# Preparing operands out of order, and scaling first halves on ScalarE, in a two-layer hybrid trunk

## The chip, the cores and the metric

The kernel runs on one core of one Trainium2 chip. The metric is the device time of one execution in microseconds (us). The engines are TensorE (PE, with weight loads shown as PEld), VectorE (DVE), ScalarE (ACT), GpSimd (POOL) and SyncE (SP, which here only issues transfers).

## What is computed

Two layers act on `x` of 1024 frames x 1024 channels in float32. Each layer is a mixer, a cross attention into 256 memory tokens, and a SwiGLU feed-forward block (FFN), each after an RMS norm and added to `x`:

```python
for layer in range(DEPTH):                 # 2
    h = rms_norm(x, g_mix[layer])
    x = x + (even_mixer(h, ...) if layer % 2 == 0 else odd_mixer(h, ...))
    m = rms_norm(mem, g_mem[layer])
    x = x + memory_cross_attention(rms_norm(x, g_xa[layer]), m, ...)   # 4 heads x 128
    x = x + swiglu(rms_norm(x, g_ffn[layer]), ...)                     # 1024 -> 2816 -> 1024

def swiglu(h, w_gate, w_up, w_down):
    return (jax.nn.silu(h @ w_gate) * (h @ w_up)) @ w_down
```

The even mixer joins a chunked spatial gating with a forgetting attention, the odd one a multi-scale pooling with a short gated convolution.

## The kernel before, in words

**Products.** Every float32 product is made of three PE products of a reduced type. An operand is split into a high half, cast by ACT, and a low half, the source less the high half, made by DVE in the helper `low` (L522). So each operand costs one ACT and one DVE instruction before PE can use it. The high and low halves live in `arena_r` (R), raw data in `arena_f` (F). Each arena has a region "a" and a region "b"; a string such as "ba" names the regions to try, in order.

**FFN blocks.** The FFN uses a seven-product scheme for 2 x 2 blocks. A `Unit` is one 1 MB block of weights (w_gate, w_up or w_down): one raw tile, loaded by one transfer (L225, on SP for gate and up, on POOL for down), from which seven `Part` objects are made by DVE adds (L236), ACT casts (L245) and DVE low halves (L522). Its raw tile is freed once part 6 is made. On the other side a `Pair` holds two row blocks of `x`, and its `Operand` objects are the combinations of its halves (L316 to L326, and the casts L330). They are ready only once the cross attention has added its result into `x` (L1764, a DVE addition), once `x_final` has stored the half to `xs` (L1833, on SP), squared it (L1839, L1850 or L1853 on ACT, summed by L1856 on POOL), and, for first halves, multiplied it in place by the norm's gain (L1861 on POOL, two tasks after). `collected` empties PE's banks (L1920 and L1951 on DVE, the latter in the down phase; L1922, L1928, L1930 on ACT). `gated` computes silu times the norm's scale (L1971 DVE, L1972 ACT, L1973 POOL), `upped` multiplies by the up branch (L1980 DVE), and `store` turns the result into the seven operands of the down phase (L2005 differences on POOL, L2009 casts on ACT, L522, then the transfer L2013 to the scratch tensor `pq` on SP). In the down phase those come back by L364. Gate and up run over 11 column blocks j of 256, gate then up; the last, j = 10, may only use region "b".

**What sets the order.** The program is a list of tasks. `Trunk.run` emits them one after the other and, ahead of each, prepares operands that later tasks need: in the order of their first use, as long as no more than `la` columns are ahead. The first operand that is not ready, or has no room, ends the round, whatever stands behind it. Raw tiles are fetched ahead too, while `held()`, the raw tiles whose first part is not yet made, is below `raws` (2 in gate and up, 4 and then 2 in the down phase) and `f_reserve` columns of F stay free. A scheduler then orders each engine's instructions by these priorities, so the order on an engine follows when `run` emitted them and not the time.

At the start of layer 1, `L742` (DVE) with `L741` and `L753` (ACT) and `L754` (POOL) makes the eight normed chunks of `x` that the odd mixer's projection reads, and `L640` (ACT) with `L522` prepares its weights.

In the listings below and in the diff, line numbers of the changed kernel differ: L245 is L256 there, L225 is L236, L522 is L551, L742 is L791, L1951 is L2004, L2013 is L2066, L364 is L386, L1718 and L1742 (the softmax's and the mix's casts) are L1767 and L1791, L1696 is L1745, L640 is L688, L1657 and L1661 (the queries) are L1706 and L1710.

## Time and profile before

| | |
|---|---|
| time, median of 3 | 2429.78 us (2426.87 to 2430.73) |
| profiled execution | 2428.93 us, span 2427.2 us |
| mean granted PE clock | 0.988 |
| PE busy | 2352.7 us, 97% |
| DVE busy | 1708.3 us, 70% |
| ACT busy | 1019.5 us, 42% |
| POOL busy | 752.7 us, 31% |

Times inside the profile count from the span's start. The FFN of layer 0 runs from about 650 us (its first stretch beside the end of the cross attention) to 1300, that of layer 1 from about 1720 on; the gate and up phase of layer 0 ends near 1150. PEclk is the share of the full clock that TensorE was granted in a stretch. A wait is put down to the engine and line that came last.

### The profile page before, as it was taken

The page shows a single profiled execution, that of the slowest core. Times are in us where ns is not written, and L with a number is a line of the kernel's source. Part 1 is how long each engine was busy: PE and PEld are TensorE (multiplying, and loading weights), DVE is VectorE, ACT ScalarE, POOL GpSimd, SP SyncE. Part 2 cuts the span into 40 slices and gives each one's busy share as a digit, 9 for nine tenths or more (in the row PEclk, how much of TensorE's full clock was granted, in tenths as well). Part 3 has the DMA queues.
Part 4 walks back from the last instruction along what each step waited for, and adds up shares of the span by engine and source line. Part 5 has one row for each costly group of instructions (what it writes and reads, how often), then busy time and mean ns, then how long its engine had stood idle before and what let it go on. Part 6 is the DMA issues. An engine that isn't in the chain of part 4 may idle for free.

```text
span 2427.2 us, 31163 instructions
## 1 busy us (share of the span) xinstructions
PE 2352.7 (97%) x11358; PEld 1981.8 (82%) x11358; DVE 1708.3 (70%) x2505; ACT 1019.5 (42%) x1850; POOL 752.7 (31%) x761
## 2 busy tenths in 40 slices
PE   7999999999999999998999999999989999999999
PEld 7998879888877777786888788888868777778887
DVE  5456457864888788886768653355878789878675
ACT  5345366745444344443323321145544444434221
POOL 6541233343334333432011310043433333342000
PEclk9999999999999999999999999999999999999999
DMA  7336335430224344337883121021223444347883
GB/s 231 118 131 210 97 91 136 130 123 18 100 83 148 130 156 156 130 116 248 295 271 124 53 78 52 27 68 45 105 80 137 142 145 148 122 165 257 275 286 101
DMA packets 227074, 335.57 MB, mean 138 GB/s; under 512 B 12864, under 2 KB 128664, under 8 KB 226920
## 3 DMA queue, kind: packets, MB, share of 16 engines
q1 hardware_dynamic: 214544, 289.32, 36.4%
q0 software_dynamic: 12192, 44.21, 5.2%
q8 instruction: 89, 1.46, 0.3%
q14 instruction: 65, 0.53, 0.1%
q10 hardware_dynamic: 184, 0.05, 0.0%
HBM read 226.44 MB, written 107.09 MB: 137 GB/s over the span
## 4 chain that ended last, share of the span: by engine, by line
PE 72%; DVE 12%; DMA 7%; issue 4%; POOL 2%; ACT 2%; SPq 0%; DVEq 0%; ACTq 0%; POOLq 0%
PE psum_t L510 69%; DVE arena_r L522 6%; DMA arena_f<-w_gate 2%; DMA arena_f<-w_up 2%; DMA pq<-arena_r 2%; DVE arena_f L236 1%; DVE arena_f L1920 1%; POOL arena_f L2005 1%; PE psum_t L1391 1%; DVE arena_f L1980 1%; ACT arena_r L245 1%; DMA arena_f<-e_w_in 1%; PE psum_t L1714 1%; DVE arena_f L1764 1%; DVE arena_r L742 0%
## 5 line engine op out<-in xcount | busy, mean ns | idle before, releaser
L510 PE MATMUL psum_t<-arena_r 128*128 128x512 f32 (+4 forms) x10304 | 2268.0, 379 | 57.8 <-DVE arena_r L522 25.2
L510 PEld LDWEIGHTS psum_t<-arena_r 128*128 128x128 f32 (+1 forms) x10304 | 1859.3, 190 | 413.9 <-DVE arena_r L522 41.8
L522 DVE TENSOR_TENSOR arena_r<-arena_f,arena_r 128x512 fp32r<-128x512 f32 (+4 forms) x803 | 662.8, 847 | 175.0 <-PE psum_t L510 47.2
L245 ACT CAST arena_r<-arena_f 128x512 fp32r<-128x512 f32 (+2 forms) x504 | 283.2, 583 | 422.7 <-PE psum_t L510 244.1
L1973 POOL TENSOR_TENSOR arena_f<-arena_f 128x512 f32<-128x512 f32 x88 | 164.3, 1873 | 475.2 <-ACT arena_f L1972 475.2
L236 DVE TENSOR_TENSOR arena_f<-arena_f 128x512 f32<-128x512 f32 (+2 forms) x288 | 207.7, 724 | 92.1 <-DMA arena_f<-w_down 53.2
L1920 DVE TENSOR_TENSOR arena_f<-psum_t,arena_f 128x512 f32<-128x512 f32 x208 | 141.0, 683 | 52.8 <-PE psum_t L510 33.7
L2009 ACT CAST arena_r<-arena_f 128x512 fp32r<-128x512 f32 x140 | 86.8, 621 | 161.0 <-DVE arena_f L1980 62.6
L2005 POOL TENSOR_TENSOR arena_f<-arena_f 128x512 f32<-128x512 f32 x80 | 132.2, 1672 | 46.2 <-DVE arena_f L1980 44.6
L1951 DVE TENSOR_TENSOR arena_f<-psum_t,arena_f 128x512 f32<-128x512 f32 x160 | 105.5, 683 | 41.8 <-PE psum_t L510 41.5
L640 ACT CAST arena_r<-arena_f 128x1024 fp32r<-128x1024 f32 (+1 forms) x57 | 59.0, 1043 | 111.4 <-PE psum_t L510 98.7
L522 DVE TENSOR_TENSOR arena_r<-psum_t,arena_r 128x512 fp32r<-128x512 f32 (+3 forms) x124 | 84.5, 703 | 22.1 <-ACT arena_r L1718 8.6
L754 POOL TENSOR_TENSOR arena_f<-arena_f 128x1024 f32<-128x1024 f32 x21 | 60.9, 2902 | 122.9 <-ACT arena_f L753 68.7
L1972 ACT ACTIVATE arena_f<-arena_f 128x512 f32<-128x512 f32 x88 | 55.6, 632 | 90.0 <-DVE arena_f L1971 89.8
L225 POOL DMA_DIRECT2D arena_f<-w_down x38 | 30.4, 800 | 181.3 <-DVE arena_r L522 101.8
L1381 POOL TENSOR_SCALAR arena_f<-arena_f,small 128x640 f32<-128x640 f32 (+6 forms) x64 | 48.4, 766 | 110.6 <-DVE small L1380 110.4
L1980 DVE TENSOR_TENSOR arena_f<-arena_f 128x512 f32<-128x512 f32 x88 | 72.6, 825 | 5.9 <-POOL arena_f L1973 1.8
L1971 DVE TENSOR_TENSOR arena_f<-arena_f 128x512 f32<-128x512 f32 x88 | 68.7, 781 | 4.2 <-ACT arena_f L782 4.1
L533 POOL TENSOR_TENSOR small<-small,mhalf 128x4 f32<-128x4 f32 (+1 forms) x64 | 63.5, 992 | 5.2
L1376 ACT ACTIVATE arena_f<-psum_t,small 128x640 f32<-128x640 f32 (+6 forms) x64 | 47.5, 745 | 23.7 <-DVE small L1374 20.7
L2206 POOL TENSOR_TENSOR arena_f<-arena_f 128x1024 f32<-128x1024 f32 x4 | 10.4, 2605 | 139.6 <-DVE arena_f L2158 134.8
L1930 ACT COPY arena_f<-psum_t 128x512 f32<-128x512 f32 x52 | 30.3, 584 | 55.0 <-PE psum_t L510 47.2
(192 smaller groups left out, 1549.8 us busy)
## 6 DMA issues: line engine op xcount, KB each, us to landing
pq<-arena_r SPq DMA_DIRECT2D x140, 512.0 KB
arena_r<-pq SPq DMA_DIRECT2D x280, 256.0 KB
arena_f<-w_gate SPq DMA_DIRECT2D x22, 1024.0 KB
arena_f<-w_up SPq DMA_DIRECT2D x22, 1024.0 KB
arena_r<-qk SPq DMA_DIRECT2D x48, 256.0 KB
qk<-arena_r POOLq DMA_DIRECT2D x16, 512.0 KB, 4.2
arena_f<-xa_wkv SPq DMA_DIRECT2D x16, 512.0 KB
arena_f<-xs SPq DMA_DIRECT2D x16, 512.0 KB
```

The costliest lines, as they stand in the source:

```text
L236: getattr(T.nc, self.adds).tensor_tensor(out=out, in0=a, in1=b, op=what)
L245: T.nc.scalar.copy(out=hv, in_=src)
L510: self.nc.tensor.matmul(out=out, lhsT=lhsT, rhs=rhs, start=start, stop=stop, skip_group_check=again)
L522: getattr(self.nc, eng).tensor_tensor(out=out, in0=src, in1=high, op=ALU.subtract)
L533: self.nc.gpsimd.tensor_tensor(out=out, in0=in_, in1=self.mhalf[:, 0:in_.shape[-1]], op=ALU.pow)
L1920: nc.vector.tensor_tensor(out=o, in0=bank[q].ap, in1=o if other is None else other, op=ALU.add)
L1951: nc.vector.tensor_tensor(out=o, in0=bank[q].ap, in1=o, op=ALU.add)
L1971: nc.vector.tensor_tensor(out=q, in0=q, in1=r, op=ALU.mult)
L1973: nc.gpsimd.tensor_tensor(out=q, in0=q, in1=r, op=ALU.mult)
L1980: nc.vector.tensor_tensor(out=c[j].ap[:, o], in0=c[j].ap[:, o], in1=s.ap[:, o], op=ALU.mult)
L2005: nc.gpsimd.tensor_tensor(out=out, in0=a, in1=b, op=ALU.subtract)
L2009: nc.scalar.copy(out=t.ap[:, 0:512], in_=src)
```

## The change

`run` no longer prepares strictly in order. `choose` takes the operand that is due, or else the first of the next 64 that is ready; an operand that is not ready is passed over. Columns of parts made ahead are limited to `parts_max`, 4608. An age test (`self.age`) is there too; every assignment in the program sets it to 0. Raw tiles are counted in `live` from their load until they are freed, and `raws` is 3 (in the down phase 4, then 3). After the cross attention's last use of the normed input, `parts_early` widens `la` to 9216 and sets `f_reserve` to 3072. The first gate and up blocks (j = 0) may put their parts in region "a" first. The scaling of first halves is an ACT activation with a scale (line 1914) in place of POOL's L1861.

```diff
@@ Part (other operand classes: aged = 0, loaded returns i)
+    aged = 1
+
+    def loaded(self, i):
+        at = self.unit.parts[0].fetched
+        return i if at is None else at
...
@@ Unit.make
         if i == 6:
             self.raw.free()
             self.tmp.free()
+            T.live -= 1
@@ Trunk
+        self.age = self.live = self.parts = 0
+        self.parts_max = 4608
@@ Trunk.run
-        def held():
-            return sum(w.heavy for w in order[npre:nd])
+        def fetch_ahead(i):
+
+            for w in pending[:160]:
+                if w.fetched is not None:
+                    continue
+                if w.heavy and self.live >= self.raws:
+                    break
+                if w.fetch(self, False):
+                    w.fetched = i
+                    self.live += w.heavy
+                elif w.ready():
+                    break
+
+        def choose(i):
+            if pending and pending[0].first <= i:
+                return pending[0], True
+            for w in pending[:64]:
+                if w.ready() and i - w.loaded(i) >= self.age * w.aged and self.parts + w.cols * w.aged <= self.parts_max:
+                    return (w, False) if ahead + w.cols <= self.la else (None, False)
+            return None, False
+
         for i, t in enumerate(self.tasks):
             self.settle()
             while True:
-                need = npre < len(order) and order[npre].first <= i
-                if not need and not (npre < len(order) and ahead + order[npre].cols <= self.la):
+                w, need = choose(i)
+                if w is None:
                     break
-                w = order[npre]
-                if not w.ready():
-                    assert not need, ("not ready", i)
-                    break
...
@@ cross attention
+        def parts_early():
+            self.la, self.f_reserve, self.age = 9216, 3072, 0
+
...
                     self.add(free_all)
+                    self.add(parts_early)
@@ x_final
         def scale():
-            nc.gpsimd.tensor_scalar(out=x, in0=x, scalar1=pr.g[e], scalar2=1.0, op0=ALU.mult, op1=ALU.mult)
+            nc.scalar.activation(out=x, in_=x, func=AF.Copy, scale=pr.g[e])
             pr.lo[e] = True
         self.defer(scale, 2)
@@ ffn
-            self.reserve, self.raws = 0, 2
+            self.reserve, self.raws = 0, 3
             self.f_reserve = 4096
...
-            g = Unit(wg, [(0, 4)], 4, j * 256, "b" if j == 10 else "ba")
-            u = Unit(wu, [(0, 4)], 4, j * 256, "b" if j == 10 else "ba")
+            g = Unit(wg, [(0, 4)], 4, j * 256, "b" if j == 10 else "ba", "ba" if j else "ab")
+            u = Unit(wu, [(0, 4)], 4, j * 256, "b" if j == 10 else "ba", "ba" if j else "ab")
...
             if n == 1:
-                self.add(lambda: setattr(self, "raws", 2))
+                self.add(lambda: setattr(self, "raws", 3))
```

The instructions of both programs are the same in number and kind, but for the sixteen scalings; what changes is where they stand. Three places follow.

First, ACT at the end of layer 0's cross attention, where the first weight parts of the FFN are cast. Before, the first of these casts (L245) stand behind the last softmax rows (L1696):

```order
L1718 CAST arena_r<-psum_t 128x1024
L1696 ACTIVATE arena_f,small<-psum_t,small 128x256 x4
L1742 CAST arena_r<-psum_t 128x512
L1718 CAST arena_r<-psum_t 128x1024
L245 CAST arena_r<-arena_f 128x512 x3
L1742 CAST arena_r<-psum_t 128x512
L1718 CAST arena_r<-psum_t 128x1024
L245 CAST arena_r<-arena_f 128x512
L1850 ACTIVATE arena_f<-arena_f 128x512
L245 CAST arena_r<-arena_f 128x512
L1853 ACTIVATE arena_f<-arena_f 128x512
```

Now nine of them (L256) stand ahead of the last softmax rows (L1745):

```order
L256 CAST arena_r<-arena_f 128x512 x5
L1706 ACTIVATE arena_r<-psum_t,gc 128x512
L688 CAST arena_r<-arena_f 128x1024
L256 CAST arena_r<-arena_f 128x512
L1791 CAST arena_r<-psum_t 128x512
L1710 ACTIVATE arena_f<-psum_t 128x512
L1767 CAST arena_r<-psum_t 128x1024
L256 CAST arena_r<-arena_f 128x512
L1745 ACTIVATE arena_f,small<-psum_t,small 128x256 x4
L256 CAST arena_r<-arena_f 128x512 x2
L1791 CAST arena_r<-psum_t 128x512
L1745 ACTIVATE arena_f,small<-psum_t,small 128x256 x4
```

The nine parts have moved ahead by about two of the softmax's row blocks; their low halves on DVE moved with them.

Second, SP at the end of gate and up in layer 0, where the last w_gate and w_up blocks are loaded among the stores to `pq`. Before:

```order
L2013 DMA pq<-arena_r 128x2x512 x11
L225 DMA arena_f<-w_gate 128x8x256
L2013 DMA pq<-arena_r 128x2x512 x7
L225 DMA arena_f<-w_up 128x8x256
L364 DMA arena_r<-pq 128x512 x110
```

Now:

```order
L2066 DMA pq<-arena_r 128x2x512 x12
L236 DMA arena_f<-w_gate 128x8x256
L2066 DMA pq<-arena_r 128x2x512 x3
L236 DMA arena_f<-w_up 128x8x256
L2066 DMA pq<-arena_r 128x2x512 x3
L386 DMA arena_r<-pq 128x512
```

Between the last two weight loads three stores are left of seven.

Third, DVE at the start of layer 1, where the sixth, seventh and eighth chunks of the normed input (L742, now L791) stand among the last evacuations of the down phase (L1951, now L2004) and the low halves of the odd mixer's weights (128x1024). Before:

```order
L522 TENSOR_TENSOR arena_r<-arena_f,arena_r 128x1024 x2
L1951 TENSOR_TENSOR arena_f<-psum_t,arena_f 128x512 x2
L522 TENSOR_TENSOR arena_r<-arena_f,arena_r 128x1024
L742 SCALAR_TENSOR_TENSOR arena_r<-arena_f,gc,arena_r 128x8x128
L1951 TENSOR_TENSOR arena_f<-psum_t,arena_f 128x512
L742 SCALAR_TENSOR_TENSOR arena_r<-arena_f,gc,arena_r 128x8x128
L522 TENSOR_TENSOR arena_r<-arena_f,arena_r 128x1024
L742 SCALAR_TENSOR_TENSOR arena_r<-arena_f,gc,arena_r 128x8x128
```

Now, from the fifth chunk on:

```order
L551 TENSOR_TENSOR arena_r<-arena_f,arena_r 128x1024 x2
L2004 TENSOR_TENSOR arena_f<-psum_t,arena_f 128x512
L551 TENSOR_TENSOR arena_r<-arena_f,arena_r 128x1024
L2004 TENSOR_TENSOR arena_f<-psum_t,arena_f 128x512
L791 SCALAR_TENSOR_TENSOR arena_r<-arena_f,gc,arena_r 128x8x128
L2004 TENSOR_TENSOR arena_f<-psum_t,arena_f 128x512 x2
L791 SCALAR_TENSOR_TENSOR arena_r<-arena_f,gc,arena_r 128x8x128
L551 TENSOR_TENSOR arena_r<-arena_f,arena_r 128x1024
L2004 TENSOR_TENSOR arena_f<-psum_t,arena_f 128x512
L791 SCALAR_TENSOR_TENSOR arena_r<-arena_f,gc,arena_r 128x8x128 x2
```

One low half of 1024 columns has moved to a place ahead of the seventh chunk here, and one more further up; the eighth chunk now follows the seventh directly.

More of the change, by code (lines that the diff above doesn't have):

```diff
@@ L546, in run @@
                     order.append(w)
-        nd = npre = 0
+        pending = order
+        for w in order:
+            w.fetched = None
         ahead = 0
-        def held():
-            return sum(w.heavy for w in order[npre:nd])
+        def fetch_ahead(i):
[16 more added lines that the diff above has]
+            return None, False
         for i, t in enumerate(self.tasks):
@@ L570, in run @@
                     break
-                npre += 1
+                pending.remove(w)
                 ahead += w.cols
-                while nd < len(order) and held() < self.raws and order[nd].fetch(self, False):
-                    nd += 1
-            while nd < len(order) and held() < self.raws and order[nd].fetch(self, False):
-                nd += 1
+                self.parts += w.cols * w.aged
+                fetch_ahead(i)
+            fetch_ahead(i)
             self.urgent(t.fn, t.boost)
@@ L580, in run @@
                     ahead -= w.cols
+                    self.parts -= w.cols * w.aged
                     w.first = -1
@@ L2070, in down_start @@
             self.x = [None] * KD
-            self.reserve, self.la, self.f_reserve, self.raws = 0, 4096, 2048, 4
+            self.reserve, self.la, self.f_reserve, self.raws, self.age = 0, 4096, 2048, 4, 0
         self.add(down_start)
@@ L2119, in down_end @@
         def down_end():
-            self.la, self.reserve = 3072, 0
+            self.la, self.reserve, self.age = 3072, 0, 0
         for n, (mp, lo, hi) in enumerate(VISITS):
@@ L2131, in ffn @@
             if n == 1:
-                self.add(lambda: setattr(self, "raws", 2))
+                self.add(lambda: setattr(self, "raws", 3))
+            if n == 3:
+                self.add(lambda: setattr(self, "age", 0))
             if 5 <= n < 9:
```

19 lines of the change are left out of this document (17 added, 2 removed).

## The prediction

> **What bounds the kernel now.** I read the page first: what share of the span TensorE (PE) is busy, and the chain that ended last.
>
> ```profile
> span 2427.2 us, 31163 instructions
> PE 2352.7 (97%) x11358; PEld 1981.8 (82%) x11358; DVE 1708.3 (70%) x2505; ACT 1019.5 (42%) x1850; POOL 752.7 (31%) x761
> PE psum_t L510 69%; DVE arena_r L522 6%; DMA arena_f<-w_gate 2%; DMA arena_f<-w_up 2%; DMA pq<-arena_r 2%; DVE arena_f L236 1%; DVE arena_f L1920 1%; POOL arena_f L2005 1%; PE psum_t L1391 1%; DVE arena_f L1980 1%; ACT arena_r L245 1%; DMA arena_f<-e_w_in 1%; PE psum_t L1714 1%; DVE arena_f L1764 1%; DVE arena_r L742 0%
> ```
>
> PE is the bound, and the change takes no matmul away, so only time that PE loses can be won. The second view, busy time by stretches of 50 us, says where it loses any.
>
> ```profile
> core 0: us, PE busy (x) PEld busy (x) DVE busy (x) ACT busy (x) POOL busy (x), PEclk, DMA share, GB/s
> 550.00:600.00 50.00, 50.00 (x290) 43.80 (x289) 21.88 (x35) 27.53 (x68) 16.25 (x35) 1.00 0.07 22
> 600.00:650.00 50.00, 50.00 (x253) 42.43 (x253) 39.75 (x61) 23.26 (x47) 15.37 (x24) 1.00 0.23 79
> 650.00:700.00 50.00, 46.86 (x218) 39.03 (x218) 45.15 (x56) 24.13 (x43) 26.75 (x19) 0.90 0.26 90
> 700.00:750.00 50.00, 47.35 (x197) 37.58 (x196) 43.00 (x58) 25.23 (x43) 19.68 (x11) 0.97 0.40 137
> 750.00:800.00 50.00, 50.00 (x222) 41.41 (x221) 41.37 (x58) 21.37 (x38) 16.75 (x9) 1.00 0.36 127
> 1050.00:1100.00 50.00, 44.42 (x190) 36.05 (x189) 39.02 (x52) 20.56 (x37) 18.90 (x13) 0.96 0.46 163
> 1100.00:1150.00 50.00, 46.69 (x197) 36.89 (x197) 34.86 (x61) 21.94 (x45) 12.83 (x12) 0.97 0.69 239
> 1300.00:1350.00 50.00, 47.71 (x208) 38.51 (x206) 46.34 (x62) 28.21 (x39) 17.64 (x7) 1.00 0.22 64
> 1350.00:1400.00 50.00, 48.22 (x208) 38.98 (x209) 28.67 (x22) 9.72 (x16) 13.36 (x16) 0.97 0.15 47
> 1700.00:1750.00 50.00, 48.52 (x234) 40.36 (x233) 42.76 (x58) 23.91 (x44) 23.29 (x20) 0.98 0.20 74
> 1750.00:1800.00 50.00, 45.92 (x193) 35.79 (x192) 38.87 (x53) 23.54 (x39) 15.54 (x11) 0.88 0.24 75
> 2150.00:2200.00 50.00, 43.64 (x178) 34.36 (x178) 37.96 (x60) 21.14 (x41) 18.10 (x13) 0.93 0.65 224
> ```
>
> An undisturbed stretch (750 to 800) holds 222 matmuls, 0.225 us each. What a stretch loses I count as its idle PE time plus (1 - PEclk) x 50 us. In 2150 to 2200 that is 6.36 + 3.5 = 9.9 us, and the 44 missing matmuls give 44 x 0.225 = 9.9 too. So: FFN opening of layer 0 (650 to 750) 3.14 + 5.0 + 2.65 + 1.5 = 12.3 us; its end (1050 to 1150) 5.58 + 2.0 + 3.31 + 1.5 = 12.4; opening of layer 1 (1700 to 1800) 1.48 + 1.0 + 4.08 + 6.0 = 12.6; its end 9.9. The start of layer 1 (1300 to 1400) loses 2.29 + 1.78 + 1.5 = 5.6. The change touches all five; the first four, 47.2 us, are the most it can win. Who is waited for, over the whole span, then in 650 to 750 and in 1700 to 1800:
>
> ```profile
> PE psum_t L510 <- DVE arena_r L522: 25.2, 27, 2.1
> PE psum_t L510 <- DVE arena_f L1920: 8.7, 2, 4.4
> ...
> PE psum_t L510 <- DVE arena_r L522: 3.4, 2, 2.1
> ...
> PE psum_t L510 <- DVE arena_r L522: 3.5, 3, 1.4
> ```
>
> In the openings it is mostly the low halves (L522) on a VectorE (DVE) that is busy 45.15 and 43.00 of 50 us, and had 28.1 idle us in 550 to 600 and 10.3 in 600 to 650. That is work made too late, not too much work.
>
> **Openings.** By the listing of the order, nine weight parts of the FFN are cast among the cross attention's softmax, where three were by the same row, so six move out of the crowded stretch; the cap of 4608 columns is nine parts of 512. Eight scalings per layer go from GpSimd (POOL) to ScalarE (ACT).
>
> ```profile
> L522 DVE TENSOR_TENSOR arena_r<-arena_f,arena_r 128x512 fp32r<-128x512 f32 x65 | 55.3, 873 | 5.6 <-ACT arena_r L2009 2.6 <-ACT arena_r L245 1.0 <-PE psum_t L510 0.8
> ...
> L236 DVE TENSOR_TENSOR arena_f<-arena_f 128x512 f32<-128x512 f32 x24 | 18.0, 758 | 5.8 <-DMA arena_f<-w_gate 5.7
> ...
> L1853 ACT ACTIVATE arena_f<-arena_f x14: 624/630/633, 638.0 to 1738.8; 128x512 f32<-128x512 f32 x14
> ...
> L1861 POOL TENSOR_SCALAR arena_f<-arena_f,gc x16: 691/1136/1662, 638.8 to 1741.4; 128x512 f32<-128x512 f32 x16
> ...
>   DMA xs<-arena_f: 0.5, 1
> ...
>   ACT arena_r L330: 8.3, 9
> ```
>
> Six parts are six low halves of 0.87 us and, with four adds to seven parts, 3.4 adds of 0.76: 7.8 us of DVE time moved ahead, into 38 us of idle time. That is more than the 3.4 us for which PE waits on L522 there (and 3.5 in layer 1), so I take those waits as gone. Half of the lost clock I give to them, since the slow steps follow clusters in which waits on ACT stand too: 3.4 + 6.5/2 = 6.6 us, and 3.5 + 7.0/2 = 7.0 us in layer 1. Bounds: nothing, if DVE stays as slow as its 0.87 us mean here, and 12.3 and 12.6. The scalings cost ACT 8 x 0.63 (an ACT instruction of this size, L1853) = 5.0 us a layer, while six casts leave; ACT idles 25 of 50 us there, and on POOL they took 1.1 us with casts (L330) behind them waiting 8.3 us in all. I cost them at nothing. Without that cover they would cost up to 5.0 us a layer.
>
> The clock needs a second look, by 10-us stretches:
>
> ```profile
> 680.00:690.00 10.00, 8.66 (x34) 7.44 (x35) 9.32 (x13) 4.75 (x9) 4.22 (x3) 0.66 0.01 2
> ...
> 1090.00:1100.00 10.00, 5.63 (x20) 4.28 (x19) 5.01 (x9) 1.58 (x3) 2.55 (x3) 0.81 0.99 337
> ...
> 1770.00:1780.00 10.00, 6.06 (x17) 3.74 (x16) 9.14 (x14) 3.38 (x6) 5.17 (x3) 0.77 0.00 0
> ```
>
> In 680 to 690 only 1.34 us are idle and yet the granted clock is 0.66; in 1090 to 1100, 4.37 idle us leave 0.81. The Trainium skill, "TensorE: Matmul & The Clock Gate", section "HAM oscillation — how this bites in real kernels", asks only that no gap exceeds some 3.4 us. By that, the short waits of the openings would cost no clock, and mending them would give none back: 6.9 us there in place of 13.6. The row of 680 to 690 speaks against it, the one of 1090 to 1100 agrees.
>
> **End of the gate and up phase.** The last w_up shares its raw tile with the last w_gate, before and after.
>
> ```profile
> 1066.62 0.37 SPq L225 DMA_DIRECT2D arena_f<-w_gate  x1
> ...
> 1092.60 1.98 SPq L225 DMA_DIRECT2D arena_f<-w_up  x1
> ...
> 1080.05 7.05 POOL L2005 TENSOR_TENSOR arena_f<-arena_f 128x512 f32<-128x512 f32 x4 [10.37 <-DVE arena_f L1980]
> ...
> 1087.13 1.14 ACT L2009 CAST arena_r<-arena_f 128x512 fp32r<-128x512 f32 x2 [0.51 <-POOL arena_f L2005]
> ...
> 1103.37 2.18 ACT L245 CAST arena_r<-arena_f 128x512 fp32r<-128x512 f32 x4 [3.10 <-DMA arena_f<-w_up]
> ...
> 1096.31 0.43 DVE L236 TENSOR_TENSOR arena_f<-arena_f 128x256 f32<-128x256 f32 x1 [4.56 <-DMA arena_f<-w_down]
> ...
> 1097.39 5.49 PE L510 MATMUL psum_t<-arena_r 128*128 128x512 f32 x12 [4.37 <-DVE arena_f L1920]
> 1104.04 3.22 PE L510 MATMUL psum_t<-arena_r 128*128 128x512 f32 x12 [1.16 <-ACT arena_r L245]
> ```
>
> DVE stands 4.56 us before an add that waits for w_down; L1920, which empties PE's bank, is queued behind it, and PE loses 4.37 us. w_up is issued at 1092.60 and used 10.8 us later. The gate's last cast stands behind ACT's L2009, which waits for POOL's four L2005 (7.05 us). In the new order that cast is not behind them, and three pq stores instead of seven stand ahead of w_up on SP. So w_up is issued up to 7.05 us earlier; it needs 4.37 + 1.16 = 5.5 us for its wait to stay hidden once the other is gone. Counted in the order of both programs, 80 matmuls (18 us) lie between what releases the first w_down loads and their use, instead of 47 (10.6 us). I take the long wait and its clock as gone, and 1.5 us (about the 1.16 us row) as what stays: 4.37 + 2.0 - 1.5 = 4.9 us; layer 1, with the same wait: 4.3 + 3.5 - 1.5 = 6.3. Together 11.2, bounds 2 (w_up comes hardly earlier) and 22.3 (all of both ends). The new order also puts POOL's L1973 ahead of those L2005; the pq stores behind those end later, and are read only in the down phase.
>
> **What is late next.** At the start of layer 1, two more low halves of 1024 columns stand on DVE ahead of the seventh L742, for which PE waits already:
>
> ```profile
> 1350.89 3.40 DVE L522 TENSOR_TENSOR arena_r<-arena_f,arena_r 128x1024 fp32r<-128x1024 f32 x1
> ...
> 1351.02 4.53 PE L510 MATMUL psum_t<-arena_r 128*128 128x512 f32 x12 [3.17 <-DVE arena_r L742]
> ```
>
> Such a low half takes up to 3.40 us beside a POOL instruction, and DVE has 3.7 idle us in 1300 to 1350 to take some of it: 0 to 6.8, and I take 3.5 us, one of them. In the tails of both cross attentions the parts made early now stand ahead of what PE's small pieces need (15 to 19 matmuls, 4 us, of lead). I charge 1.5 us each, between one and two waits of 25.2/27 = 0.93 us; bounds 0 and 5 for both. The steady middle I leave at nothing: the order keeps 49 to 65 matmuls (11 us or more) between what releases a w_up load and its use, against the 10.8 us of the slowest load.
>
> **Sum.** Against the profiled run of 2428.93 us: -6.6 - 7.0 - 11.2 + 3.5 + 3.0 = -18.3, so 2410.6. The median shown is 0.85 higher, and I say 2411. All bounds together give 2382 and 2439.
>
> **Rivals.**
> - *The clock does not come back.* The slow steps of the openings belong to something other than those waits. Then 6.75 of the 13.6 us stay: 2417. For it: 0.66 with 1.34 idle us; against it: no stretch without idle time is under 1.00. The rule of the Trainium skill named above comes out here. Chance 0.10.
> - *DVE stays the bound of the openings.* 88 of 100 us are busy; less 7.8 still 80, next to POOL, and the waits on L522 only change places: ends 11.2, losses 6.5, 2424. For it: PE's waits on L522 are spread over the whole span (27 of them), where none of this work stands. Chance 0.20.
> - *The change does less than it says.* The two last loads still share a tile, the new age test is never above zero, and the count of raw tiles is capped by space too: ends give 2, not 11.2: 2420. Chance 0.12.
> - *Slower.* SP now issues a third 1 MB load ahead of the sixteen stores to xs. Each scaling overwrites what a store reads, and sits on ACT ahead of L330's casts and the last mix's cast; POOL once waited 0.5 us for this and delayed nobody on ACT. If the stores wait for half of a 10.8 us load in each layer, the openings' 13.6 are lost and 2 x 5.4 come on top: 2435. It decides from some 3 us of delay. Against it: DMA is 0.23 busy there. Chance 0.09.
> - *All four places are mended*, 47.2 less 6.5: 2388. Chance 0.09.
>
> **How the numbers follow.** The forecast has 0.40, with 2403 to 2418 as its own range. From 2395 (most of the last case is outside) to 2429 (the slower case is outside) holds about 0.8. A measurement tells 0.2%, 4.9 us, from no change, so faster means under 2424.9. That holds for nearly all of the forecast, the clock rival and the full mending (0.57), half of the DVE rival and most of the lesser change: 0.78. Same 0.14, slower 0.08.
>
> **What would show it.** Right: in the stretches that hold the openings DVE's busy time falls by some 8 us, in the softmax stretch it rises, PEclk there is 0.95 or more; no wait on L1920 over 2 us; w_up issued 5 us or more sooner after the last w_gate than 26 us. Right for the loss: the wait on L742 is over 5 us. The forecast is wrong if PE waits on ACT's casts in the openings, if the scalings on ACT (line 1914 of the changed kernel) begin after a wait on xs, or if the down phase waits on w_down again.

## The result, and the profile after

The changed kernel takes 2389.92 us (median of 5, 2385.24 to 2391.95), the kernel before, on the same chips, 2426.87 (2424.17 to 2430.73): a ratio of 0.9846, 95% interval 0.9836 to 0.9857, some 37 us less. The prediction was 2411 us, with 2395 to 2429 as its range: the right direction, about half of the size, and the time lies 5 us under the range.

The page of the profile after, its span and busy times:

```profile
span 2388.1 us, 31149 instructions
PE 2337.4 (98%) x11358; PEld 1976.5 (83%) x11358; DVE 1705.6 (71%) x2505; ACT 1024.2 (43%) x1866; POOL 743.0 (31%) x745
```

The same 11358 matmuls stand in a span that is 39 us shorter. TensorE's (PE's) waits over the whole span, in the changed kernel (L551 is the low half, L1973 the emptying of a bank in gate and up, L791 the chunks of the odd mixer's input, L256 the cast of weight parts):

```profile
PE psum_t L539 <- DVE arena_r L551: 10.7, 15, 2.7
...
PE psum_t L539 <- DVE arena_r L791: 6.2, 2, 5.3
PE psum_t L539 <- ACT arena_r L256: 3.6, 3, 1.7
...
PE psum_t L539 <- DVE arena_f L1973: 1.5, 1, 1.5
```

The waits for low halves fell from 25.2 us to 10.7, those for the emptying of banks from 8.7 to 1.5, and the ones for the chunks rose from 3.2 to 6.2. Busy times by stretches, of the changed kernel:

```profile
550.00:600.00 50.00, 50.00 (x291) 43.80 (x289) 25.28 (x40) 27.57 (x65) 17.03 (x37) 1.00 0.13 43
...
650.00:700.00 50.00, 50.00 (x240) 41.64 (x239) 45.06 (x61) 30.45 (x52) 19.68 (x13) 0.93 0.22 78
700.00:750.00 50.00, 48.92 (x216) 40.19 (x215) 46.26 (x58) 22.35 (x40) 17.78 (x11) 1.00 0.41 144
...
1050.00:1100.00 50.00, 48.00 (x203) 38.73 (x202) 41.59 (x69) 23.64 (x47) 18.59 (x16) 0.97 0.73 255
1100.00:1150.00 50.00, 50.00 (x222) 41.40 (x222) 39.67 (x65) 21.33 (x40) 11.04 (x11) 1.00 0.80 269
...
1300.00:1350.00 50.00, 43.43 (x186) 34.54 (x185) 34.94 (x35) 14.80 (x16) 16.19 (x6) 0.93 0.25 74
```

VectorE's (DVE's) columns are the third pair. In 550 to 600 it does 3.4 us more than before. In 650 to 750 it is as busy as before (91.3 of 100 us, against 88.2): the stretch did not empty, it came to hold work that belonged later.

Both programs have the same number of PE instructions, and almost the same order, so the time between the same two of them can be compared. The table gives, for each part of the program, the profiled time less that of the kernel before (us; negative is a gain). "Start" is the part ahead of the first cross attention's tail, where all the programs are the same: its -0.3 to -5.3 is what two profiles of the same code differ by, most of it in waits for the first loads. The other parts should be read to about 1 or 2 us. The tail of layer 1 (predicted +1.5) and the last down phase have no column; they moved by nothing and by +1.2 us in the changed kernel.

| kernel | median | start | tail, layer 0 | opening 0 | steady 0 | end 0 | start of layer 1 | opening 1 | steady 1 | end 1 |
|---|---|---|---|---|---|---|---|---|---|---|
| predicted | 2411 | 0 | +1.5 | -6.6 | 0 | -4.9 | +3.5 | -7.0 | 0 | -6.3 |
| changed | 2389.92 | -2.3 | +2.5 | -10.4 | -6.6 | -8.8 | +4.1 | -10.6 | -6.6 | -1.4 |
| a_strict | 2427.08 | -0.3 | +0.1 | -0.3 | +0.3 | -2.4 | +3.2 | -6.3 | +5.9 | -2.0 |
| a_only | 2403.68 | -0.6 | +1.9 | -4.5 | -9.0 | -0.7 | -0.3 | -4.2 | -5.9 | +0.3 |
| b_scale | 2417.35 | -1.5 | 0.0 | -5.9 | -1.6 | +0.1 | -1.7 | -4.0 | +0.7 | +1.1 |
| a_noscale | 2391.54 | -5.3 | +1.1 | -5.7 | -8.2 | -9.3 | +4.9 | -8.6 | -6.4 | -2.2 |
| b_raws3 | 2429.89 | -0.6 | 0.0 | +2.1 | -4.3 | +5.2 | -0.1 | -0.9 | -10.4 | +7.8 |
| a_raws2 | 2402.23 | -2.4 | +0.8 | -8.1 | -7.9 | -1.6 | +3.9 | -8.6 | -2.2 | -0.4 |
| a_raws4f | 2388.90 | -3.2 | +0.4 | -9.4 | -4.4 | -5.0 | +3.4 | -11.9 | -9.0 | -3.0 |
| a_noearly | 2395.56 | -2.0 | +0.4 | -8.1 | -8.2 | -1.1 | +3.1 | -10.7 | -7.0 | -4.8 |
| a_early3 | 2464.57 | -1.0 | +1.5 | -6.5 | +18.2 | +3.2 | +4.7 | -2.5 | +9.3 | +6.5 |
| a_twice | 2431.51 | -1.4 | +1.1 | -9.2 | +9.6 | -5.6 | +4.0 | -9.5 | +14.4 | -3.2 |
| a_down | 2388.91 | -1.3 | +2.4 | -10.6 | -7.9 | -6.2 | +3.8 | -7.4 | -7.0 | -3.4 |
| a_spread1 | 2405.39 | -3.7 | +1.9 | -3.2 | -5.8 | -4.8 | +3.5 | -7.5 | -2.4 | -3.3 |
| a_sqv | 2376.79 | -0.5 | +2.3 | -10.6 | -7.8 | -9.0 | -2.7 | -13.4 | -6.7 | -3.5 |
| b_sqv | 2426.48 | -5.3 | 0.0 | -0.1 | -1.5 | -0.1 | -2.0 | -0.6 | +1.7 | -0.3 |

Names with a_ are the changed kernel with one thing altered, names with b_ the kernel before. The first row of results says where the prediction missed: the two openings gave 21.0 us where 13.6 were forecast, the two steady stretches 13.2 where nothing was, and the end of layer 1 gave 1.4 where 6.3 was.

### The profile page after: what moved, and what is told of

Same layout as the page of the kernel before. It is cut to its first block, busy times and chain, and to the rows that moved or that the text cites. A ratio compares the mean times of both kernels' runs of the same rounds, so it can differ in the third digit from the quotient of the medians.

```text
span 2388.1 us, 31149 instructions
## 1 busy us (share of the span) xinstructions
PE 2337.4 (98%) x11358; PEld 1976.5 (83%) x11358; DVE 1705.6 (71%) x2505; ACT 1024.2 (43%) x1866; POOL 743.0 (31%) x745
## 3 DMA queue, kind: packets, MB, share of 16 engines
q8 instruction: 89, 1.46, 0.3%
## 5 line engine op out<-in xcount | busy, mean ns | idle before, releaser
L539 PE MATMUL psum_t<-arena_r 128*128 128x512 f32 (+4 forms) x10304 | 2255.4, 378 | 34.2 <-DVE arena_r L551 10.7
L551 DVE TENSOR_TENSOR arena_r<-arena_f,arena_r 128x512 fp32r<-128x512 f32 (+4 forms) x803 | 672.1, 857 | 167.5 <-PE psum_t L539 53.2
L256 ACT CAST arena_r<-arena_f 128x512 fp32r<-128x512 f32 (+2 forms) x504 | 282.4, 584 | 429.4 <-PE psum_t L539 252.6
L1973 DVE TENSOR_TENSOR arena_f<-psum_t,arena_f 128x512 f32<-128x512 f32 x208 | 141.7, 685 | 51.6 <-PE psum_t L539 36.0
L2004 DVE TENSOR_TENSOR arena_f<-psum_t,arena_f 128x512 f32<-128x512 f32 x160 | 106.4, 686 | 36.0 <-PE psum_t L539 35.7
L803 POOL TENSOR_TENSOR arena_f<-arena_f 128x1024 f32<-128x1024 f32 x21 | 60.6, 2884 | 127.8 <-ACT arena_f L802 61.9
L551 DVE TENSOR_TENSOR arena_r<-psum_t,arena_r 128x512 fp32r<-128x512 f32 (+3 forms) x124 | 84.6, 703 | 18.7 <-ACT arena_r L1443 6.8
L2261 POOL TENSOR_TENSOR arena_f<-arena_f 128x1024 f32<-128x1024 f32 x4 | 10.4, 2598 | 139.5 <-DVE arena_f L2213 139.5
L1753 POOL TENSOR_SCALAR arena_f<-arena_f,small 128x256 f32<-128x256 f32 x64 | 33.3, 538 | 65.2 <-DVE small L1750 50.8
```

The costliest lines, as they stand in the source:

```text
L256: T.nc.scalar.copy(out=hv, in_=src)
L539: self.nc.tensor.matmul(out=out, lhsT=lhsT, rhs=rhs, start=start, stop=stop, skip_group_check=again)
L551: getattr(self.nc, eng).tensor_tensor(out=out, in0=src, in1=high, op=ALU.subtract)
L1973: nc.vector.tensor_tensor(out=o, in0=bank[q].ap, in1=o if other is None else other, op=ALU.add)
L2004: nc.vector.tensor_tensor(out=o, in0=bank[q].ap, in1=o, op=ALU.add)
```

## The experiments

### Passing over: a_strict and a_only

In a_strict operands are prepared strictly in order again, and everything else of the change stays.

```diff
-            for w in pending[:64]:
+            for w in pending[:1]:
```

> The changed kernel, but operands are prepared strictly in the order of their first use again: one that is not ready blocks all behind it. Theory A and the prediction's reading of the openings: the six parts go back into the crowded stretch, the openings lose 13 to 22 us, the steady stretches keep their gain by the third raw tile: 2403 to 2412. Theory B: the openings lose as much and the steady stretches lose 10 to 13 us with them: 2415 to 2425. A third reading (widening the columns that are prepared ahead, and the third raw tile, did it all, and passing over does nothing): 2388 to 2393.

It took 2427.08 us, 1.0001 of the kernel before (0.9991 to 1.0012): without passing over, nothing is left of the change in all. The opening of layer 0 has its loss back, and the steady stretches lose their gain with three raw tiles in place; the opening of layer 1 keeps 6.3 of its 10.6 us. None of the three readings had the sum, and the one of Theory B (below) came nearest.

The opposite test is a_only: passing over with the other edits undone. The bookkeeping that came with it (raw tiles counted until they are freed, the cap of 4608 columns) stays in both tests and has none of its own.

```diff
-            nc.scalar.activation(out=x, in_=x, func=AF.Copy, scale=pr.g[e])
+            nc.gpsimd.tensor_scalar(out=x, in0=x, scalar1=pr.g[e], scalar2=1.0, op0=ALU.mult, op1=ALU.mult)
...
-                    self.add(parts_early)
...
-            self.reserve, self.raws = 0, 3
+            self.reserve, self.raws = 0, 2
...
-            g = Unit(wg, [(0, 4)], 4, j * 256, "b" if j == 10 else "ba", "ba" if j else "ab")
+            g = Unit(wg, [(0, 4)], 4, j * 256, "b" if j == 10 else "ba")
...
-                self.add(lambda: setattr(self, "raws", 3))
+                self.add(lambda: setattr(self, "raws", 2))
```

> Passing over alone: the changed kernel with the scalings on GpSimd, two raw tiles in gate and up and after the first visit of the down phase, no widening of the columns ahead before the tail, and the first blocks' parts placed as before. If passing over carries the change (strict order gave 2427), it keeps the openings' gain in good part: 2400 to 2410. If it needs the other edits as they need it (each alone was worth 0 to 9.7 us), it stays near the kernel before: 2418 to 2428.

2403.68 us, ratio 0.9911 (0.9891 to 0.9932): more than half of the gain, from 4 us in each opening and all of the steady stretches. So passing over carries more than half of the change; a_strict has all the rest of it and gains nothing.

### The scaling: b_scale and a_noscale

```diff
-            nc.gpsimd.tensor_scalar(out=x, in0=x, scalar1=pr.g[e], scalar2=1.0, op0=ALU.mult, op1=ALU.mult)
+            nc.scalar.activation(out=x, in_=x, func=AF.Copy, scale=pr.g[e])
```

b_scale does this alone to the kernel before.

> The kernel before with only the sixteen scalings of first halves moved from GpSimd to ScalarE. The prediction's reading (they cost nothing and win nothing by themselves): 2425 to 2429. Rival (part of the openings' gain of 21.6 us came from GpSimd and from casts that no longer wait 8.3 us for it): each opening gains 3 to 5 us, 2417 to 2421.

2417.35 us, ratio 0.9960 (0.9944 to 0.9976): the sixteen scalings, which the prediction had cost at nothing, win 9.3 us by the medians, and by the table 5.9 and 4.0 us in the openings. a_noscale puts the scalings of the changed kernel back on GpSimd (POOL).

> The changed kernel with the sixteen scalings put back on GpSimd. If the scaling's 9.7 us in the kernel before (2417 against 2427) are a gain of its own that adds to the rest, both openings lose 4 to 6 us: 2398 to 2401. If passing over reaches the same by another way (parts made early leave room for whatever waits on GpSimd), little is lost: 2389 to 2394. The prediction's reading, that the scaling wins nothing, says the same as the latter.

2391.54 us (2389.66 to 2394.8), 0.9863 (0.9848 to 0.9878): only 1.6 us more than the changed kernel, or some 4 by the ratios to the kernel before, which the intervals do not tell apart. By the table the openings do lose 4.7 and 2.0 us; 1.6 us come back in the steady stretch of layer 0, and this profile's start is 3 us shorter, which is no part of the edit. The two gains do not add.

### How early the parts are made: a_noearly and a_early3

a_noearly leaves out the task that widens the columns prepared ahead (the line `self.add(parts_early)`).

> The changed kernel without the step that widens the columns prepared ahead to 9216 after the last use of the normed input; the width stays at 3072 until the tail of the cross attention. The prediction's reading of the openings (gain from work moved into the idle time of the softmax) needs this step: most of what passing over wins there goes, 5 to 6 us a layer, and the tail of layer 0 gets its 2.5 us back: 2397 to 2400. Rival: passing over alone is enough: 2388 to 2392.

2395.56 us, 0.9876 (0.9862 to 0.9891). The sum is near what the prediction's reading gave, the place is not: the openings kept 8.1 and 10.7 us, and what went is the end of layer 0 (-1.1 in place of -8.8). So that step is not what mends the openings. It does not decide whether parts are made early either: in its trace five and nine weight parts are cast ahead of the last softmax row in layers 0 and 1 (none and one before, nine and seven in the changed kernel). The profile, 2.6 us slower than the median, also has 7.7 us of loss in the last down phase, where the changed kernel has 1.2.

a_early3 allows three parts ahead (1536 columns), as many as stood there before, until the steady stretches begin.

```diff
-        self.parts_max = 4608
+        self.parts_max = 1536
...
         def steady():
-            self.reserve, self.la = 3072, 2048
+            self.reserve, self.la, self.parts_max = 3072, 2048, 4608
...
             if left == 1:
                 self.add(down_end)
+                self.add(lambda: setattr(self, "parts_max", 1536))
```

> The changed kernel with at most 1536 columns (three parts, as many as the kernel before has at that row) prepared ahead until the steady stretches of gate and up begin, and 4608 from there on. The prediction's reading (the openings gain because six parts move into the idle time of the softmax): the openings lose 10 to 14 us of their 21: 2400 to 2406. Rival (what counts is that an operand that is not ready no longer blocks those behind it, and how early the parts are made counts little): 2389 to 2394.

Both sides missed the time: 2464.57 us, 1.0165 (1.0148 to 1.0181), slower than before. The openings gained 6.5 and 2.5 us, 12.0 less than in the changed kernel, which is what the prediction's reading expected there, so fewer parts ahead do cost; but the large loss, 18.2 and 9.3 us, is in the steady stretches, where the cap is lifted. VectorE waited 28.9 and 15.6 us there for weights to land. The order in which blocks are fetched at the start of the steady stretch stays with it for most of its length: here, on SyncE, a w_up load, one store, a w_gate load and then six stores stood in this order, again and again, where the changed kernel mostly has two to five stores behind each load.

### The steady stretches: a_raws2, b_raws3, a_raws4f, a_twice

After the result I had two theories. Theory A: blocks land earlier, since three raw tiles are held, and VectorE's adds wait less. Theory B: the steady stalls before were the aftermath of a late opening. What VectorE waited for in the steady stretch of layer 0, before:

```profile
DVE arena_f L236 <- DMA arena_f<-w_gate: 10.9, 4, 4.9
...
DVE arena_f L236 <- DMA arena_f<-w_up: 3.3, 2, 2.8
```

and in the changed kernel (no such wait for w_up):

```profile
DVE arena_f L247 <- DMA arena_f<-w_gate: 7.5, 3, 3.5
```

How such a wait reaches PE is seen at the longest stall of that stretch, in the kernel before, on VectorE, then PE:

```profile
838.94 1.42 DVE L236 TENSOR_TENSOR arena_f<-arena_f 128x512 f32<-128x512 f32 x2 [4.90 <-DMA arena_f<-w_gate]
840.28 0.68 DVE L522 TENSOR_TENSOR arena_r<-arena_f,arena_r 128x512 fp32r<-128x512 f32 x1
...
841.01 13.89 PE L510 MATMUL psum_t<-arena_r 128*128 128x512 f32 x60 [1.91 <-DVE arena_r L522]
```

The low half that PE waits for stands on VectorE behind an add that waited 4.90 us for its block.

a_raws2 is the changed kernel with two raw tiles, b_raws3 the kernel before with three.

```diff
-            self.reserve, self.raws = 0, 3
+            self.reserve, self.raws = 0, 2
```

> The changed kernel with two raw weight tiles at a time in gate and up instead of three; they are still counted until they are freed. Theory A (the steady stretches of gate and up gained 6.6 us in layer 0 and 6.0 us in layer 1 because the weights of the next block land earlier): both stretches fall back, so 2390 + 10 to 14, about 2402, and VectorE waits again for w_gate in its adds by 10 us or more per layer. Theory B (the steady stalls before were the aftermath of late openings): the steady stretches keep their gain, and the time stays within 2388 to 2393. In both the openings keep their gain, since nine parts need two raw tiles only.

> The kernel before with three raw tiles instead of two in gate and up, nothing else changed. Theory A: the steady stretches gain 10 to 13 us in all, 2427 - 12 = about 2415. Theory B: the openings are as late as before, so nothing follows: 2424 to 2430.

a_raws2 took 2402.23 us, 0.9892 (0.9877 to 0.9907), which is the number of Theory A, by another way: the steady stretch of layer 0 kept its gain (VectorE waited 2.5 us for weights), that of layer 1 lost most of it (11.8 us), and the end of layer 0 lost 7.2. b_raws3 took 2429.89 us, 1.0011 (1.0000 to 1.0023), which is the number of Theory B, again by another way: the steady stretches gained 4.3 and 10.4 us, with waits of 4.5 and 1.5, and the ends lost 5.2 and 7.8. A median alone would have misled twice; the parts of the table say that the third tile matters for the landing in layer 1, and that theory B is wrong: in b_raws3 the openings are as late as before, and the steady stretches gain all the same.

a_raws4f holds four tiles and keeps less space free.

```diff
-            self.reserve, self.raws = 0, 3
-            self.f_reserve = 4096
+            self.reserve, self.raws = 0, 4
+            self.f_reserve = 2048
```

> The changed kernel with four raw weight tiles in gate and up and only 2048 columns of space kept free. If the steady stretches are set by VectorE adds that wait for weights (in the six kernels so far each us less of these waits went with some 0.8 us less time in the same stretch), the waits fall from 7.5 and 5.1 us to under 3 in each layer and the steady stretches gain 2 to 6 us more. The last w_gate and w_up again have seven stores between them in layer 0, so its end loses 4 to 7 us: 2388 to 2394 in all, with the gain in the steady stretches and the loss at the ends. Rival (the steady gain has nothing to do with the weights' landing): the steady stretches stay as they are or lose, 2394 to 2400.

2388.90 us, 0.9854 (0.9837 to 0.9870), the same as the changed kernel. The end of layer 0 lost 3.8 us, near the 4 to 7 expected, and layer 1's steady stretch won 2.4; but in layer 0 VectorE waited 17.7 us for weights, not under 3, and the stretch still was 4.4 us better than before. So the waits are not the whole of it, and in that one case they hardly show.

a_twice therefore delays the landing: from the second block on, the last left out, each load is issued twice.

```diff
-            getattr(T.nc, self.queue).dma_start(
+            for _ in range(2 if self.queue == "sync" and 256 <= self.c0 < 2560 else 1):
+                getattr(T.nc, self.queue).dma_start(
```

> The changed kernel, but each weight block of gate and up from the second on, the last left out, is loaded twice into its raw tile, the second load over the first. If the steady stretches gained because VectorE's adds wait less for weights to land, later landing brings the waits back (from 7.5 and 5.1 us to 12 us and more) and with them 4 to 12 us in each steady stretch: 2398 to 2412. If the steady gain has another cause (the openings, or the order alone), the stretches stay within 3 us: 2387 to 2394.

2431.51 us, 1.0030 (1.0016 to 1.0043). The steady stretches lost 16.2 and 21.0 us against the changed kernel, more than expected, and the rest of the table stayed within 4. VectorE's waits in that stretch of layer 0:

```profile
DVE arena_f L248 <- DMA arena_f<-w_gate: 29.0, 6, 7.3
...
DVE arena_f L248 <- DMA arena_f<-w_up: 1.3, 2, 0.7
```

Over the two steady stretches of all sixteen kept traces, 32 in number, each us of VectorE's waits for weights goes with 0.8 us of time (correlation 0.91). So the landing time is the best account of these stretches: an add waits for a block, and the low halves and the emptying of banks behind it are what PE is seen to wait for. It is not isolated, though. In a_twice VectorE's order changed too (at 174 of the 318 places of layer 0's stretch it runs another kind of instruction than the changed kernel), stores to pq stand between the doubled loads, and a_raws4f's layer 0 lies some 7 us under the line.

### The start of layer 1: a_down, a_sqv, b_sqv

a_down goes back to two raw tiles after the down phase's first visit, which puts VectorE's order there back to what it was before.

```diff
             if n == 1:
-                self.add(lambda: setattr(self, "raws", 3))
+                self.add(lambda: setattr(self, "raws", 2))
```

> The changed kernel with two raw tiles instead of three in the down phase after its first visit, as before. In the order of VectorE four low halves of 1024 columns stand ahead of the seventh chunk of the odd mixer's input, as before, instead of six. The prediction's reading of the loss there: the wait goes from 5.3 us back to 3.2 and the second half-clock step goes: 2390 - 4 = 2385 to 2387. Rival: the third raw tile also fed the down phase, which loses as much: 2389 to 2393.

2388.91 us, 0.9856 (0.9839 to 0.9872): no difference. The wait on the seventh chunk fell from 5.3 to 3.6 us, but other waits came, both half-clock steps stayed, and the part lost 3.8 us as the changed kernel does (this profile is 7 us slower than the median of its runs). So the two low halves made that wait longer, and do not by themselves make the part slow. The changed kernel there, on VectorE, then GpSimd and PE:

```profile
1308.40 1.22 DVE L551 TENSOR_TENSOR arena_r<-arena_f,arena_r 128x1024 fp32r<-128x1024 f32 x1
...
1322.32 3.40 DVE L551 TENSOR_TENSOR arena_r<-arena_f,arena_r 128x1024 fp32r<-128x1024 f32 x1
...
1326.24 6.07 DVE L791 SCALAR_TENSOR_TENSOR arena_r<-arena_f,gc,arena_r 128x1024 fp32r<-128x1024 f32 x2
...
1321.30 9.93 POOL L803 TENSOR_TENSOR arena_f<-arena_f 128x1024 f32<-128x1024 f32 x3 [4.17 <-ACT arena_f L802]
...
1329.07 3.35 PE L539 MATMUL psum_t<-arena_r 128*128 128x512 f32 x7 [5.29 <-DVE arena_r L791]
```

The same low half takes 1.22 us alone and 3.40 beside GpSimd's additions (L803, 9.93 us for three). Those add up the squares for the norm, which is not needed yet. a_sqv moves these seven additions to VectorE.

```diff
-    def chunk_sq(self, k):
+    def chunk_sq(self, k, eng="gpsimd"):
...
-            nc.gpsimd.tensor_tensor(out=self.ssq.ap, in0=self.ssq.ap, in1=sq.ap, op=ALU.add)
+            getattr(nc, eng).tensor_tensor(out=self.ssq.ap, in0=self.ssq.ap, in1=sq.ap, op=ALU.add)
...
-                        self.chunk_sq(k)
+                        self.chunk_sq(k, "vector")
```

> The changed kernel with the seven additions of squares (1024 columns, 3.3 us each on GpSimd) of the odd mixer's norm moved to VectorE (1.2 us each by its other instructions of that size). In the profile of the changed kernel a VectorE instruction of 1024 columns takes 1.2 us alone and 2.8 to 3.4 beside one of those additions. If the wait of 5.3 + 0.9 us at the start of layer 1 comes from that overlap, it falls below 3 us, one half-clock step goes with it: 2390 - 5 = 2383 to 2387. If it comes from the two more low halves on VectorE, as the prediction had it, seven more instructions there make it longer: 2392 to 2397.

2376.79 us (2375.06 to 2378.3), 0.9797 (0.9780 to 0.9815): faster than both kernels. The two waits on L791 are 1.55 and 0.43 us, and no half-clock step is left there. VectorE in its profile:

```profile
1317.90 1.21 DVE L803 TENSOR_TENSOR arena_f<-arena_f 128x1024 f32<-128x1024 f32 x1
1319.04 2.47 DVE L791 SCALAR_TENSOR_TENSOR arena_r<-arena_f,gc,arena_r 128x1024 fp32r<-128x1024 f32 x2
1321.43 1.21 DVE L551 TENSOR_TENSOR arena_r<-arena_f,arena_r 128x1024 fp32r<-128x1024 f32 x1
```

Two chunks take 2.47 us where they took 6.07. The part itself won 6.8 us; of the rest, 4.9 us are in the opening and end of layer 1, where VectorE's order changed too. Each of the two has one half-clock step less there (those from 1722 and 2156 us in the changed kernel), 3.4 us in all; why was not tested. b_sqv does the same to the kernel before.

> The kernel before, with only the seven additions of squares at the start of layer 1 moved from GpSimd to VectorE. If their overlap with VectorE's 1024-column instructions is a cause by itself, the kernel before loses its wait of 3.2 us on the seventh chunk and its half-clock step there too: 4 to 7 us less, 2417 to 2420. If it needs the two more low halves of the changed kernel to show, the kernel before stays at 2422 to 2427.

2426.48 us, 1.0003 (0.9992 to 1.0015): no difference, though its profile shows that part 2.0 us shorter (it was 3.2 us of wait, and one of 0.8 stayed). The overlap costs at most 2.0 us in the kernel before and 6.8 us in the changed one; what differs between them there is the order, so it seems to take both: the additions on GpSimd, and the low halves that the new order puts beside them.

### The clock of the openings: a_spread1

The changed kernel, by 10-us stretches:

```profile
660.00:670.00 10.00, 10.00 (x47) 8.42 (x48) 9.96 (x12) 4.41 (x9) 4.73 (x4) 0.83 0.14 53
...
680.00:690.00 10.00, 10.00 (x41) 8.19 (x41) 8.92 (x15) 4.26 (x8) 5.38 (x3) 0.83 0.01 2
```

PE is busy in all of both, and yet the granted clock is 0.83. Just ahead of each stands a lot of one-column matmuls, which sum squares:

```profile
658.38 2.82 PE L539 MATMUL psum_t<-ones,arena_f 128*128 128x1 f32 x24
...
677.96 2.73 PE L539 MATMUL psum_t<-ones,arena_f 128*128 128x1 f32 x24
```

a_spread1 defers these matmuls one by one, which puts them into lots of other sizes.

```diff
-            self.defer(sums)
+            for b in range(4):
+                self.defer(lambda b=b: sums(b), 1 + b)
```

> The changed kernel with the four one-column matmuls of each channel block's sum of squares deferred one by one; in TensorE's order they then stand in lots of 5, 4, 4 and 23 in layer 0, instead of 12, 4, 8 and 12. If the half-clock steps of the opening come from waits, as the prediction had it, the opening of layer 0 keeps its two steps or fewer (6.8 us at half clock). If they come from lots of one-column matmuls, in which TensorE counts as busy and hardly works, the lot of 23 (some 5 us) brings two steps or more right behind it and with no wait ahead of them, and the lots of 4 and 5 bring none.

One execution: 2405.39 us, 15 us slower than the changed kernel, which the table puts mostly into the openings, the end of layer 0 and the steady stretch of layer 1. The lot of 23 (46 entries in the trace, two for each matmul):

```profile
675.12 8.66 PE L539 MATMUL psum_t<-ones,arena_f 128*128 128x1 f32 x46
```

and the stretches around it:

```profile
660.00:670.00 10.00, 10.00 (x49) 8.36 (x49) 8.65 (x12) 4.73 (x8) 2.73 (x2) 1.00 0.07 27
670.00:680.00 10.00, 8.21 (x42) 6.69 (x41) 8.89 (x10) 5.21 (x9) 4.84 (x4) 0.84 0.32 105
680.00:690.00 10.00, 10.00 (x39) 8.78 (x40) 9.71 (x15) 4.08 (x8) 5.48 (x4) 0.65 0.01 2
```

The clock is halved from 677 to 687 us, three steps in a row, and the lot of 4 at 667.58 brought none. In layer 1 the lot of 23 (from 1746.20 us) brought three steps too. Waits of 1.46 and 1.14 us stand just ahead of these two, so they are not free of waits; but the two lots of the changed kernel above are.

Yet not every such lot halves the clock. a_twice has the same two lots, and keeps the full clock in all of its opening of layer 0:

```profile
659.50 2.73 PE L540 MATMUL psum_t<-ones,arena_f 128*128 128x1 f32 x24
...
660.00:670.00 10.00, 10.00 (x59) 8.71 (x60) 9.96 (x15) 7.01 (x13) 3.39 (x3) 1.00 0.19 72
...
676.60 2.73 PE L540 MATMUL psum_t<-ones,arena_f 128*128 128x1 f32 x24
...
680.00:690.00 10.00, 7.41 (x30) 5.18 (x29) 8.10 (x13) 3.56 (x7) 5.53 (x4) 1.00 0.10 32
```

The clock records of the sixteen kept traces show the difference. In each trace all half-clock steps begin a whole number of 3.41 us apart, on a grid whose place in the program differs between runs. For each cell of this grid behind the first 12 us (ahead of them idle cells brought no step) I added PE's idle time and its one-column time. Of the cells at full clock, 85 hold 2.13 us or more, and every one was followed by a half-clock cell; of 270 with 1.15 to 2.13 us, 49 were; of 10640 with less, none. The lots of the changed kernel put 2.51 and 2.73 us into one cell. Those of a_twice are cut by the grid, into 0.97 and 1.76 us and into 0.94 and 1.79. So waits and one-column matmuls count alike, and where a lot falls on the grid differs from run to run: a part of the clock's gain can be luck.

## Why the prediction was right or wrong

**Where PE's time can be won** held in part. PE stayed the bound, but "the first four, 47.2 us, are the most it can win" left out the steady stretches. In the rows of 50 us from 800 to 1050 and from 1800 to 2150 us, of which these two lose most, PE of the kernel before is idle for 17.0 us, and 13.2 of the 39 us were won there:

```profile
1800.00:1850.00 50.00, 47.47 (x208) 38.43 (x207) 43.70 (x59) 20.86 (x38) 20.96 (x11) 1.00 0.38 136
...
1900.00:1950.00 50.00, 47.21 (x206) 38.08 (x205) 40.20 (x56) 21.55 (x39) 16.83 (x10) 1.00 0.47 158
```

**The openings** were mis-sized, and their reason was half wrong. The step that failed first is "I cost them at nothing", on the scalings: alone they won 5.9 and 4.0 us, and in the changed kernel they are worth 4.7 and 2.0 (a_noscale), most of the 7.4 us by which the openings passed the forecast. The row for it was quoted, the 8.3 us for which casts waited behind GpSimd; the prediction used it as cover and not as a gain. The second is that moving six parts into the softmax's idle time wins the waits on L522. How many parts are cast ahead of the last softmax row does not by itself decide: with none and two in the two layers a_only won 4.5 and 4.2 us, with five and five a_strict won 0.3 and 6.3, while a_early3, held to three, fell 12.0 short of the changed kernel. DVE's time in 650 to 750 did not fall by 8 us, as the prediction said it would, but rose by 3. That the forecast of 6.6 and 7.0 us comes near the 5.7 and 8.6 of a_noscale is therefore partly luck. One of its signs of being wrong did come: two scalings began behind waits on xs, 1.6 us together.

**The clock** was read wrongly. The half of the lost clock that went to waits was the guess of the prediction; "no stretch without idle time is under 1.00" holds for its rows of 50 us only. In the kernel before PE is busy in all of 690 to 700 us, and the granted clock is 0.83: the second and third step there follow a lot of one-column matmuls (5.11 us from 683.96), and the row of 680 to 690, with its 1.34 us of idle time, holds that lot. The steps follow such lots and crowded waits alike. The rival that the clock does not come back was wrong in what it forecast, and right that something other than waits is in it. Eight steps in the openings before (three from 683 us, one each from 734, 1748 and 1762, two from 1775; 27.3 us at half clock) became three (from 661, 681 and 1722; 10.2 us), so 8.5 us came back, more than the 6.75 that the prediction took. The Trainium skill, "TensorE: Matmul & The Clock Gate", section "HAM oscillation — how this bites in real kernels", looks for gaps in which PE is idle. The two stretches of the changed kernel shown above have none, so here the rule misses the case, and the measurement decides.

**The end of gate and up** was right in the main part of its mechanism. In the changed kernel, on SyncE, then PE:

```profile
1047.20 0.37 SPq L236 DMA_DIRECT2D arena_f<-w_gate  x1
...
1069.09 0.37 SPq L236 DMA_DIRECT2D arena_f<-w_up  x1
...
1076.36 3.94 PE L539 MATMUL psum_t<-arena_r 128*128 128x512 f32 x10 [1.73 <-ACT arena_r L256]
```

w_up follows w_gate after 21.9 us, where it took 26.0, 4.1 us sooner and not the 5 that the prediction had asked as its sign. What stays is a wait of 1.73 us on a cast, where the prediction left 1.5. In layer 0 the term was too small, 4.9 against 8.8 us, since the two waits further on (0.58 and 1.57 us) and 1.20 before them went too. In layer 1 it was too large, 6.3 against 1.4: the wait on the emptying of a bank went from 4.3 to 1.5, but a new one of 2.73 us came.

```profile
2147.34 1.33 ACT L256 CAST arena_r<-arena_f 128x256 fp32r<-128x256 f32 x4 [2.09 <-DMA arena_f<-w_down]
...
2153.92 2.69 DVE L551 TENSOR_TENSOR arena_r<-arena_f,arena_r 128x256 fp32r<-128x256 f32 x7
...
2155.62 4.60 PE L539 MATMUL psum_t<-arena_r 128*128 128x512 f32 x12 [2.73 <-DVE arena_r L551]
...
2180.74 119.56 PE L539 MATMUL psum_t<-arena_r 128*128 128x512 f32 x526 [1.48 <-DVE arena_f L1973]
```

The parts of the first w_down block are made late there, behind a wait for its landing: the prediction had named that as what would make it wrong. The price of the third raw tile at this place is tied to passing over: it is worth 7 us at the end of layer 0 when operands are passed over (a_raws2), and costs 5 when they are not (b_raws3).

**The steady stretches** are the step that failed most: "the steady middle I leave at nothing", where 13.2 us were won. It held the slowest load against the number of matmuls between what releases a load and PE's use. But the first to need the load is VectorE's add, ahead of all that VectorE has to do behind it, and the 14.2 us that VectorE waited there before in layer 0 were in the trace. With the loads issued twice these stretches lost 16 and 21 us (a_twice). Why passing over makes the blocks land earlier there, where all weight parts are ready, is not shown: the order at the entry to the stretch seems to persist (a_early3), and with four tiles in layer 0 the waits and the time disagree (a_raws4f). This stays open.

**The start of layer 1** was right in size, +3.5 against +4.1, and half right in its reason: the two low halves lengthened that wait (a_down), but they cost what they do because they fall beside GpSimd's additions (a_sqv). That overlap as the cause rests on the rows and on a_sqv, which moved VectorE's order with it, and in the kernel before the same edit won nothing in the median (b_sqv). The prediction had the row, 3.40 us beside a POOL instruction, and took it as a bound and not as the cause. The tails cost 2.5 and nothing, against 1.5 each.

**The rivals.** Full mending of the four places, 2388 us, had a chance of 0.09 and came nearest in time; but by another sum, with the end of layer 1 unmended and the steady stretches in its place. The slower rival found no support but the 1.6 us of waits on xs: the scalings on ScalarE won time.

## What to carry to other kernels

A load's lead is to be measured against the first instruction that waits for it, not against the matmul that uses its result: here an add that waited 4.90 us for a block held up the low half behind it, and PE with it. A prefetcher that stops at the first operand which is not ready couples things that have nothing to do with each other; passing over it was worth 20 us without the other edits. What an edit is worth depends on the others: the scalings won 9.3 us alone and 2 to 4 beside the rest, the third raw tile nothing alone and 11 to 12 beside the rest, so parts should be tried in both directions. And where two engines slow each other, moving work that is not urgent off the second one can win more than reordering the first.

## What the runs showed of the hardware

- PE's half-clock steps lie on a grid of 3.41 us. With PE busy all the time, a cell that held 2.13 us or more of 128x1 matmuls was followed by a half-clock cell in 18 of 18 cases in the sixteen traces, one with 1.9 to 2.13 us in 3 of 12, one with 0.2 to 1.9 us in none of 450. Lots of 2.82 and 2.73 us did it in the changed kernel; two of 2.73 us in a_twice, each cut by the grid, did not.
- A VectorE instruction of 128x1024 took 1.2 us alone and 2.8 to 3.4 us beside a GpSimd addition of the same size, which itself took 3.3 us there, and 2.4 (at 1298.80) where VectorE ran instructions of 256 columns.
